# A row-sum kernel whose first row per partition becomes a block of its own: 128 contiguous rows, then blocks of 111 and 16 rows per partition

## The chip, the cores and the metric

The kernel runs on one core of a Trainium2 chip. The metric is device time in microseconds (us), the median of repeated runs. The profile comes from one further execution.

## The reference

```python
batch, seq, dim = 32, 512, 1024
x = np.random.randn(batch, seq, dim).astype(np.float32)

def reference(x):
    return np.sum(x, axis=-1).astype(np.float32)
```

There are 32 x 512 = 16384 rows of 1024 float32 numbers (4 KB a row, 67.1 MB in all), and the output is one float32 sum for each row.

## The kernel before

The 16384 rows are spread over 128 partitions, 128 rows to a partition, in two blocks. In the body block partition p holds the 112 consecutive rows from 112p on (`x_a`, `out_a`); in the end block it holds the 16 rows from 128 x 112 + 16p on (`x_z`, `out_z`). So two neighbouring partitions of the body lie 112 rows, 448 KB, apart in device memory, and two of the end block 64 KB.

The body is loaded in seven steps of 16 rows per partition (8.39 MB) into three buffers `xt0` to `xt2` in turn. Each step is two loads from SyncE's queue (SP), one for the even and one for the odd partitions, 64 partitions each, both counted on the semaphore of the buffer (`slots`). Step 0 is split once more: a small load of the first row of each partition (128 x 1024, semaphore `first`) goes ahead, and the two large loads bring the other 15 rows. The end block is loaded in pieces of 9, 4 and 2 rows (`CUTS`) into the next buffer, and its last row in two parts of 544 and 480 columns into `tail`. All 20 loads are issued by one loop (L138) in this order; from step 3 on SP waits until VectorE (DVE) has freed the buffer (`freed`, counted on `vec`). The first three loads (`EARLY = 3`) are moved by hand ahead of the barrier at the program's start.

VectorE waits for `first`, then for each step in turn, and reduces the 16 rows of a step with one instruction (L55) into `res_a`. Of step 6 it takes 9 rows, and ScalarE (ACT) takes the other 7, one instruction a row (L66). ScalarE then waits for all of these and issues the stores of `res_a` (L115) as three DMAs of 104, 12 and 12 partitions. Its part of the end block is behind these in its program: 5 of the 9 rows of piece 0, 2 of the 4 rows of piece 1, and 1 of the 2 rows of piece 2. VectorE takes the other rows; the last two rows are halved and added in pairs (L73), the very last one in its two parts. SP waits for ScalarE's and VectorE's counts (L139, L140), issues the store of `res_z` (L141), waits for `early_store`, clears the semaphores and waits for its store (L146).

```python
for i, k in ((0, 104), (104, 116), (116, P)):
    nc.scalar.dma_start(out=out_a[i:k], in_=res_a[i:k]).then_inc(sems["early_store"], 16)
```

Of the kernel before, what the change touches and what calls it, by code (L numbers as in the profile page):

```python
# [6 lines left out]
COPY = mybir.ActivationFunctionType.Copy  # L7
X = mybir.AxisListType.X

BODY = 112  # L10
G = 16
BUFS = 3
ACT_ROWS = 7
CUT = 544
# [4 lines left out]
def row_sums(nc, x: bass.AP, out: bass.AP):  # L19
    P = nc.NUM_PARTITIONS  # L20
    x_flat = x.flatten_outer_dims()
    R, D = x_flat.shape
    C = R // P
    assert R % P == 0 and C == BODY + G and BODY % G == 0
    out_flat = out.rearrange("a (b c) -> (a b c)", c=1)

    def block(r0, n):
        x_b = x_flat[r0 : r0 + P * n].rearrange("(p c) d -> p (c d)", p=P)
        out_b = out_flat[r0 : r0 + P * n].rearrange("(p c) -> p c", p=P)
        return x_b, out_b  # L30

    x_a, out_a = block(0, BODY)
    x_z, out_z = block(P * BODY, G)

    def sbuf(name, n):
        return nc.alloc_sbuf_tensor(name, [P, n], F32)

    xt = [sbuf(f"xt{i}", G * D) for i in range(BUFS)]
    tail = sbuf("tail", D + 16)
    pairs = [sbuf(f"pairs{i}", D // 2) for i in range(3)]  # L40
    res_a = sbuf("res_a", BODY)
    res_z = sbuf("res_z", G)

    names = [f"slot{i}" for i in range(BUFS)] + ["first", "piece0", "piece1", "piece2", "tail0"]
    names += ["tail1", "vec", "act", "early_store", "store"]
    sems = {n: nc.alloc_semaphore(n) for n in names}
    slots = [sems[f"slot{i}"] for i in range(BUFS)]
    vec, act = sems["vec"], sems["act"]
    numbers = [s.num for s in sems.values()]
    assert numbers == list(range(numbers[0], numbers[0] + len(numbers)))  # L50

    count = {"vec": 0, "act": 0}

    def rows_dve(t, j, n, res, c):
        nc.vector.tensor_reduce(  # L55
            out=res[:, c : c + n],
            in_=t[:, j * D : (j + n) * D].rearrange("p (j d) -> p j d", d=D),
            axis=X,
            op=ADD,
        ).then_inc(vec, 1)  # L60
        count["vec"] += 1

    def rows_act(t, j, n, res, c):
        for i in range(n):
            v = t[:, (j + i) * D : (j + i + 1) * D]
            nc.scalar.activation(  # L66
                out=v, in_=v, func=COPY, accum_out=res[:, c + i : c + i + 1]
            ).then_inc(act, 1)
            count["act"] += 1

    def pairs_dve(t, a, b, acc, pairs):
        h = (a + b) // 2
        nc.vector.tensor_tensor_reduce(  # L73
            out=pairs[:, 0 : h - a], in0=t[:, a:h], in1=t[:, h:b], scale=1.0, scalar=0.0,
            op0=ADD, op1=ADD, accum_out=acc,
        ).then_inc(vec, 1)
        count["vec"] += 1

    n_bufs = BODY // G


    freed = {}
    loads = []
    for b in range(n_bufs):
        c = b * G
        parts = [(q, 0, slots[b % BUFS]) for q in (slice(0, P, 2), slice(1, P, 2))]
        if b == 0:
            parts = [(slice(0, P), 0, sems["first"])] + [(q, 1, s) for q, i, s in parts]
        for q, i, s in parts:
            k = 1 if s is sems["first"] else G  # L90
            loads.append((b, xt[b % BUFS][q, i * D : k * D], x_a[q, (c + i) * D : (c + k) * D], s))
    last = xt[n_bufs % BUFS]
    for k, (i, j) in enumerate(zip(CUTS, CUTS[1:])):
        loads.append((n_bufs, last[:, i * D : j * D], x_z[:, i * D : j * D], sems[f"piece{k}"]))
    for k, (i, j, gap) in enumerate(((0, CUT, 0), (CUT, D, 16))):
        e = (G - 1) * D
        loads.append((0, tail[:, i + gap : j + gap], x_z[:, e + i : e + j], sems[f"tail{k}"]))


    nc.vector.memset(tail[:, CUT + 15 : CUT + 16], 0.0).then_inc(vec, 1)  # L100
    count["vec"] += 1
    nc.vector.wait_ge(sems["first"], 16)
    for b in range(n_bufs):
        a = ACT_ROWS if b == n_bufs - 1 else 0
        nc.vector.wait_ge(slots[b % BUFS], 32 * (b // BUFS + 1))
        rows_dve(xt[b % BUFS], 0, G - a, res_a, b * G)
        freed[b] = count["vec"]
        if a:
            nc.scalar.wait_ge(slots[b % BUFS], 32 * (b // BUFS + 1))
            rows_act(xt[b % BUFS], G - a, a, res_a, b * G + G - a)  # L110
    body_vec, body_act = count["vec"], count["act"]
    nc.scalar.wait_ge(vec, body_vec)
    nc.scalar.wait_ge(act, body_act)
    for i, k in ((0, 104), (104, 116), (116, P)):
        nc.scalar.dma_start(out=out_a[i:k], in_=res_a[i:k]).then_inc(sems["early_store"], 16)  # L115

    for k in range(2):
        i, j = CUTS[k], CUTS[k + 1]
        h = (j - i) // 2
        nc.vector.wait_ge(sems[f"piece{k}"], 16)  # L120
        rows_dve(last, i, h, res_z, i)
        nc.scalar.wait_ge(sems[f"piece{k}"], 16)
        rows_act(last, i + h, j - i - h, res_z, i + h)
    nc.scalar.wait_ge(sems["piece2"], 16)
    rows_act(last, 14, 1, res_z, 14)
    nc.vector.wait_ge(sems["piece2"], 16)
    pairs_dve(last, 13 * D, 14 * D, res_z[:, 13:14], pairs[2])
    nc.vector.wait_ge(sems["tail0"], 16)
    pairs_dve(tail, 0, CUT, tail[:, CUT + 14 : CUT + 15], pairs[0])
    nc.vector.wait_ge(sems["tail1"], 16)  # L130
    nc.vector.wait_ge(vec, count["vec"])  # L131
    pairs_dve(tail, CUT + 14, D + 16, res_z[:, 15:16], pairs[1])


    for b, dst, src, s in loads:
        if b >= BUFS:
            nc.sync.wait_ge(vec, freed[b - BUFS])
        nc.sync.dma_start(out=dst, in_=src).then_inc(s, 16)  # L138
    nc.sync.wait_ge(vec, count["vec"])  # L139
    nc.sync.wait_ge(act, count["act"])  # L140
    nc.sync.dma_start(out=out_z, in_=res_z[:, :]).then_inc(sems["store"], 16)  # L141


    nc.sync.wait_ge(sems["early_store"], 48)
    nc.sync.sem_clear(range(numbers[0], sems["store"].num))
    nc.sync.wait_ge(sems["store"], 16).then_inc(sems["store"], -16)  # L146


def kernel(tc: tile.TileContext, x: bass.AP, out: bass.AP):
    tc.close()  # L150
    tc.compile()  # L151
    nc = tc.nc
    row_sums(nc, x, out)

    sp = mybir.EngineType.SP
    fn = nc.m.functions[0]
    entry, body = None, None
    for blk in fn.blocks:  # L160
        ops = [i for i in blk.instructions if i.engine == sp]
        if entry is None:
            entry = blk
        elif any(i.opcode == "DMACopy" for i in ops):
            body = blk
            break
    code = list(body.instructions)
    loads = [i for i in code if i.engine == sp and i.opcode == "DMACopy"][:EARLY]
    for load in loads:
        assert not load.sync_info.on_wait  # L170
        code.remove(load)
    body.instructions = code
    code = list(entry.instructions)
    at = next(k for k, i in enumerate(code) if i.engine == sp and i.opcode == "Drain")
    code[at:at] = loads
    entry.instructions = code
# [29 lines left out]
```

## Time and profile before

| | |
|---|---|
| median of 3 runs | 160.85 us (160.85 to 160.98) |
| the profiled execution's own time | 160.87 us |
| its span in the profile | 159.5 us |
| DVE busy | 121.3 us (76%), 16 instructions |
| ACT busy | 17.1 us (11%), 31 instructions |
| DMA | 67.18 MB, mean 421 GB/s over the span |
| SP's queue (q1) | 2128 packets, 97.8% of 16 engines' span |
| ACT's queue (q10) | 165 packets, 0.1% |

The span runs from the first recorded instruction to the last one; the rest of the execution's time, 160.87 - 159.5 = 1.3 us, lies around it. A q1 packet is one partition's piece of a load (or of the last store), or the 4-byte write that counts the load as complete on one of the 16 DMA engines. "Idle before" an instruction tells how long its engine waited, and for what.

### The profile page before, as it was taken

Reading aid. Unit: us, or ns where it says so; the run is one execution under the profiler, and the core shown is the slowest. Engines: PE = TensorE matmul, PEld = TensorE weight load, DVE = VectorE, ACT = ScalarE, POOL = GpSimd, SP = SyncE. Lnnn points to the kernel's source line nnn. Section 1 sums busy time; section 2 is a strip of 40 time slices with the busy share of each in tenths; the row PEclk is TensorE's granted clock in tenths of the full one; section 3 lists DMA queues with packets and bytes.
Section 4 is the critical chain, followed back from the end, with each engine's and each line's share of the span. In section 5 each row is a group of like instructions: output and inputs, shape, how many; then the busy total and the mean of one; then the engine's idle time right before and its main releaser. Section 6 shows DMA issues by size and latency. Waiting matters only on the chain.

```text
span 159.5 us, 116 instructions
## 1 busy us (share of the span) xinstructions
DVE 121.3 (76%) x16; ACT 17.1 (11%) x31; POOL 0.2 (0%) x4
## 2 busy tenths in 40 slices
DVE  0000049998699968999599994999949999499785
ACT  2000000000000000000000000000000000394595
POOL 0000000000000000000000000000000000000000
DMA  9979996996996989979969969969969979799993
GB/s 378 493 308 431 493 509 279 526 509 279 526 493 296 526 378 411 526 329 460 526 296 493 526 279 509 526 263 526 509 279 526 460 329 526 305 434 444 395 411 131
DMA packets 2293, 67.18 MB, mean 421 GB/s; under 512 B 629, under 2 KB 757, under 8 KB 1013
## 3 DMA queue, kind: packets, MB, share of 16 engines
q1 hardware_dynamic: 2128, 67.12, 97.8%
q10 hardware_dynamic: 165, 0.06, 0.1%
HBM read 67.11 MB, written 0.07 MB: 421 GB/s over the span
## 4 chain that ended last, share of the span: by engine, by line
DMA 73%; DVE 23%; SPq 1%; issue 0%; DVEq 0%
DMA xt<-in_x_dram 73%; DVE res_a L55 22%; SPq L138 1%; DVE pairs L73 1%; DVEq L131 0%; DVE tail L73 0%; DVE res_z L73 0%
## 5 line engine op out<-in xcount | busy, mean ns | idle before, releaser
L55 DVE TENSOR_REDUCE res_a<-xt 128x16 f32<-128x16384 f32 (+1 forms) x7 | 113.1, 16153 | 31.7 <-DMA xt<-in_x_dram 31.7
L66 ACT ACTIVATE xt<-xt 128x1024 f32<-128x1024 f32 x15 | 15.6, 1041 | 137.7 <-DMA xt<-in_x_dram 137.7
L55 DVE TENSOR_REDUCE res_z<-xt 128x4 f32<-128x4096 f32 (+1 forms) x2 | 6.7, 3353 | 1.6 <-DMA xt<-in_x_dram 1.6
L66 ACT ACTIVATION_READ_ACCUMULATOR xt<-xt 128x1 f32 x15 | 2.8, 186 | 0.0
L100 DVE MEMSET tail<- 128x1 f32 x1 | 0.1, 59 | 3.0 <-PEq L151 3.0
L66 ACT ACT_TABLE_LOAD x1 | 1.3, 1283 | 2.9 <-PEq L151 2.9
L73 DVE CUSTOM_DVE_ANT_0 pairs<-tail 128x272 f32<-128x272 f32 (+1 forms) x2 | 0.8, 424 | 0.1
L73 DVE CUSTOM_DVE_ANT_0 pairs<-xt 128x512 f32<-128x512 f32 x1 | 0.7, 694 | 0.3 <-DMA xt<-in_x_dram 0.3
L73 DVE DVE_READ_ACCUMULATOR2_ANT res_z<- 128x1 f32 x2 | 0.2, 82 | 0.0
L190 POOL MEMSET const-bfloat16-1.0<- 128x1 bf16 x1 | 0.1, 101 | 0.0
L190 POOL MEMSET const-uint8-127<- 128x1 uint8 x1 | 0.1, 101 | 0.0
L190 POOL MEMSET const-float32-0.0<- 128x1 f32 x1 | 0.1, 98 | 0.2 <-issue 0.2
L190 POOL MEMSET const-float32-1.0<- 128x1 f32 x1 | 0.1, 98 | 0.0
L73 DVE DVE_READ_ACCUMULATOR2_ANT tail<- 128x1 f32 x1 | 0.1, 82 | 0.0
## 6 DMA issues: line engine op xcount, KB each, us to landing
xt<-in_x_dram SPq DMA_DIRECT2D x2, 3840.0 KB, 16.6
xt<-in_x_dram SPq DMA_DIRECT2D x1, 4608.0 KB, 32.4
xt<-in_x_dram SPq DMA_DIRECT2D x1, 2048.0 KB, 36.9
xt<-in_x_dram SPq DMA_DIRECT2D x1, 1024.0 KB, 39.0
xt<-in_x_dram SPq DMA_DIRECT2D x1, 512.0 KB, 3.8
tail<-in_x_dram SPq DMA_DIRECT2D x1, 272.0 KB, 39.1
tail<-in_x_dram SPq DMA_DIRECT2D x1, 240.0 KB, 39.2
xt<-in_x_dram SPq DMA_DIRECT2D x12, 39.0
```

The costliest lines, as they stand in the source:

```text
L55: nc.vector.tensor_reduce(out=res[:, c : c + n], in_=t[:, j * D : (j + n) * D].rearrange("p (j d) -> p j d", d=D), axis=X, op=ADD,).then_i ...
L66: nc.scalar.activation(out=v, in_=v, func=COPY, accum_out=res[:, c + i : c + i + 1]).then_inc(act, 1)
L73: nc.vector.tensor_tensor_reduce(out=pairs[:, 0 : h - a], in0=t[:, a:h], in1=t[:, h:b], scale=1.0, scalar=0.0, op0=ADD, op1=ADD, accum_out ...
L100: nc.vector.memset(tail[:, CUT + 15 : CUT + 16], 0.0).then_inc(vec, 1)
L138: nc.sync.dma_start(out=dst, in_=src).then_inc(s, 16)
L190: nc = _bacc.Bacc("TRN2", target_bir_lowering=False, num_devices=1)
```

## The change

The first row of each partition is taken out of the body. A new block, `x_h` and `out_h`, holds rows 0 to 127 of the whole input, one to a partition, so that its load reads 512 KB that lie in one piece. The body starts at row 128 with 111 rows per partition (steps of 15, 16, 16, 16, 16, 16, 16 rows); the end block stays where it was. VectorE reduces the new block with an instruction of its own into `res_h`, and step 0 then has 15 rows instead of 16. ScalarE issues a fourth store, `res_h` to `out_h` (128 partitions, 4 bytes each), behind the three of `res_a`, and `early_store` is waited for at 64 instead of 48. The neighbouring partitions of the body lie 444 KB apart instead of 448 KB. Number, order and sizes of the 20 loads stay the same.

```diff
-BODY = 112
+BODY = (15, 16, 16, 16, 16, 16, 16)
+HEAD = 1
+END = 16
...
-    x_a, out_a = block(0, BODY)
-    x_z, out_z = block(P * BODY, G)
+    x_h, out_h = block(0, HEAD)
+    x_a, out_a = block(P * HEAD, N)
+    x_z, out_z = block(P * (HEAD + N), END)
...
-        c = b * G
+        c = starts[b]
         parts = [(q, 0, slots[b % BUFS]) for q in (slice(0, P, 2), slice(1, P, 2))]
-        if b == 0:
-            parts = [(slice(0, P), 0, sems["first"])] + [(q, 1, s) for q, i, s in parts]
+        m = HEAD if b == 0 else 0
+        if m:
+            loads.append((b, xt[b][:, 0 : m * D], x_h, sems["first"]))
         for q, i, s in parts:
-            k = 1 if s is sems["first"] else G
-            loads.append((b, xt[b % BUFS][q, i * D : k * D], x_a[q, (c + i) * D : (c + k) * D], s))
+            k = BODY[b]
+            loads.append((b, xt[b % BUFS][q, m * D : (m + k) * D], x_a[q, c * D : (c + k) * D], s))
...
     nc.vector.wait_ge(sems["first"], 16)
+    rows_dve(xt[0], 0, HEAD, res_h, 0)
     for b in range(n_bufs):
         a = ACT_ROWS if b == n_bufs - 1 else 0
         nc.vector.wait_ge(slots[b % BUFS], 32 * (b // BUFS + 1))
-        rows_dve(xt[b % BUFS], 0, G - a, res_a, b * G)
+        rows_dve(xt[b % BUFS], 0 if b else HEAD, BODY[b] - a, res_a, starts[b])
...
     for i, k in ((0, 104), (104, 116), (116, P)):
         nc.scalar.dma_start(out=out_a[i:k], in_=res_a[i:k]).then_inc(sems["early_store"], 16)
+
+    nc.scalar.dma_start(out=out_h, in_=res_h[:, :]).then_inc(sems["early_store"], 16)
...
-    nc.sync.wait_ge(sems["early_store"], 48)
+    nc.sync.wait_ge(sems["early_store"], 64)
```

## The prediction

> **What bounds the kernel now.** I read the page's queues and chain first, then the timeline of the end, then the start in windows of 0.25 us, and last the packet records behind these views. Queue and chain:
>
> ```profile
> q1 hardware_dynamic: 2128, 67.12, 97.8%
> q10 hardware_dynamic: 165, 0.06, 0.1%
> DMA xt<-in_x_dram 73%; DVE res_a L55 22%; SPq L138 1%; DVE pairs L73 1%; DVEq L131 0%; DVE tail L73 0%; DVE res_z L73 0%
> ```
>
> SP's load queue keeps all 16 DMA engines at work for 97.8% of the span. The chain also names the VectorE reductions (L55), but that is only because a freed buffer releases an issue. The next lines show that these releases cost nothing:
>
> ```profile
> 41.25 17.22 DVE L55 TENSOR_REDUCE res_a<-xt 128x16 f32<-128x16384 f32 x1 [2.06 <-DMA xt<-in_x_dram]
> 60.60 17.22 DVE L55 TENSOR_REDUCE res_a<-xt 128x16 f32<-128x16384 f32 x1 [2.13 <-DMA xt<-in_x_dram]
> ...
> 149.22 1.06 ACT L66 ACTIVATE xt<-xt 128x1024 f32<-128x1024 f32 x1 [3.83 <-DMA xt<-in_x_dram]
> ...
> 157.46 0.18 ACT L66 ACTIVATION_READ_ACCUMULATOR xt<-xt 128x1 f32 x1
> 157.63 0.41 DVE L73 CUSTOM_DVE_ANT_0 pairs<-tail 128x241 f32<-128x241 f32 x1
> 157.97 0.08 DVE L73 DVE_READ_ACCUMULATOR2_ANT res_z<- 128x1 f32 x1
> 158.08 0.35 SPq L141 DMA_DIRECT2D out_dram<-res_z  x1
> ```
>
> VectorE waits 2.1 us for every step: 8.39 MB each 19.35 us, 433 GB/s. In the packet records a 65,536-byte packet takes 2.418 us at the median (27.1 GB/s an engine, 433.6 GB/s for 16), a 61,440-byte one 2.267, and packets follow one another without gaps from about 3 us to 157.08. So the end is fixed by when the slowest engine gets into its stride, plus the bytes, plus whatever else it carries. Behind that comes a tail: the last load lands 39.2 us after its issue at 118.35, at 157.55; VectorE's last pair of rows starts at 157.63 and ends at 158.05; SP's store follows at 158.08. ScalarE ends at 157.64, so it has 0.4 us to spare.
>
> The start is the only stretch where the engines are not in stride:
>
> ```profile
> 0.75:1.00 0.25, 0.00 (x0) 0.00 (x0) 0.00 (x0) 1.00 0.00 0
> 1.00:1.25 0.25, 0.00 (x0) 0.00 (x0) 0.00 (x0) 1.00 1.62 164
> 1.25:1.50 0.25, 0.00 (x0) 0.00 (x0) 0.00 (x0) 1.00 0.53 82
> 1.50:1.75 0.25, 0.00 (x0) 0.00 (x0) 0.00 (x0) 1.00 0.26 98
> 1.75:2.00 0.25, 0.00 (x0) 0.00 (x0) 0.00 (x0) 1.00 0.80 246
> 2.00:2.25 0.25, 0.00 (x0) 0.00 (x0) 0.00 (x0) 1.00 1.06 393
> 2.25:2.50 0.25, 0.00 (x0) 0.00 (x0) 0.00 (x0) 1.00 1.03 426
> ```
>
> The last column is GB/s, counted by packets in the stretch where they start. From 1.0 to 2.0 us it is 82 to 246 instead of over 400. This is the 128-packet first load. Its records: 4096 bytes take 159 ns at the median, but 218 ns in the mean and up to 994 ns; the slow ones are each engine's first packets, which start between 1.02 and 1.43 us. The excess is 8 x (218.3 - 159) ns = 0.47 us per engine in the mean. The 16 completions of this load spread from 2.63 to 3.40 us; the latest engine stalled twice (842 and 591 ns) and ends last at 157.08 too.
>
> **The change part by part.**
>
> **The contiguous first load.** It is still 128 packets of 4096 bytes, 8 to an engine, and SP issues it in the same place, so issue (0.38 us) and bytes stay. What moves is the addresses: engines read 32 KB apart within 512 KB, instead of one row every 448 KB. An engine ends 157.08 - 3.40 = 153.68 us after its first completion if it carries no store. An engine that carries stores takes 8.84 - 8.65 = 0.19 us longer from piece 0's completions to the last load's (147.91 to 156.75 against 148.43 to 157.08). 104 rows lie on 13 engines and 12 on 12 (128 rows + 37 completions = the 165 packets of q10), so three engines have none.
> Without stalls a first completion comes at 1.02 + 8 x 0.159 = 2.29 us for the first engine and 1.43 + 1.27 = 2.70 for the last. If all the stall stays, it comes at 3.40 as now. Does the stall come from scattered addresses, or from a cold start that any first packet meets? For addresses: the latest engine's very first packet (at 1.015, 156 ns) was quick, and its second and third, 448 KB on each, were not. Against: at 136.8 us the end block's untouched memory is entered, and the first 36,864-byte packets keep to 1.364 to 1.372 us; there, though, work was queued ahead. I take half of the mean stall as staying: 2.70 + 0.24 = 2.94 for the latest engine.
>
> [...]
>
> **The fourth store, on the DMA engines.** 128 packets of 4 bytes and 16 completions, 9 per engine. The nearest rows are the 4-byte completions, 9 ns, and the 64-byte packets of the `res_z` store, 8 to 11 ns: 9 x 9 = 0.08 us per engine. Below zero is excluded, since the packets stand between loads on busy engines. The upper end is the 448-byte packets' 25 ns: 0.23 us. I take 0.08, the row nearest in size. Rows of `res_a` become 444 instead of 448 bytes, for which I add nothing up to 10 x 25 ns = 0.25 us should a packet double. The queue alternates with SP's: the present stores run from 151.2 to 155.76, and the new packets then fit between the 16 packets of the two tail loads (88 and 79 ns), so they are done by about 156.7. SP looks at `early_store` only at 158.48, so that wait is covered by some 1.5 us.
>
> [...]
>
> **The fourth store, on ScalarE.** The three issues take 1.38 us from 147.79 and already hold ScalarE until 149.22, though piece 0 was there for VectorE at 148.92. From there ScalarE goes without a pause to 157.64, so the new issue delays everything queued behind it: 8 rows, and SP's L140 that waits for them. Nearest rows: 0.31, 0.38 and 0.62 us for the three, 0.35 for the 128-partition store of `res_z`. I take 0.38 + 0.03 between issues = 0.41; ends 0.34 and 0.65. ScalarE then ends at 158.05 (157.98 to 158.29) against VectorE's 158.05: nothing to +0.25 us, and nothing taken, because the cover of 0.40 us is just used up. A gain at the start moves both ends alike.
>
> **VectorE.** One more reduction of one row at about 4 us, 1.1 to 1.2 us by 9.75 us for 9 rows and 2.29 for 2. It lies inside the 18.96 us that VectorE waits for step 0. Step 0's reduction becomes 17.22 - 1.08 = 16.14 us. SP's issue of step 3, at 39.22, comes some 1.1 us earlier; nobody waits, since the engines reach step 3 only at 59.4, when step 2's completions come. Nothing.
>
> **The body at 444 KB pitch.** Packet counts and sizes are equal. Rows now start on multiples of 4 KB instead of 64 KB; so do the 61,440-byte packets and the pieces now, and they run at 27 GB/s. Nothing; no gain either, since no packet has a gap to give up. The price if wrong is the slower rival.
>
> Sum: latest store engine 2.94 + 0.19 + 0.08 + 153.68 = 156.89 against 157.08, -0.19 us; the tail follows. 160.87 - 0.19 = 160.68 for the profiled execution, 160.66 by the median, which is 0.02 lower; I say 160.65.
>
> **Rivals.**
> *The stall moves or stays.* The stretches after the contiguous load are new memory for step 0's 60 KB rows, and the stall could fall there, or it was a cold start. For it: ten or more of the 16 first packets were slow, whatever their address. Then only the store's 0.08 us is left, at most 0.25 with ScalarE last: 160.95.
> *All of the stall goes.* 2.70 + 0.19 + 0.08 + 153.68 = 156.65, -0.43 us: 160.4.
> *Slower: the rows that no longer start on 64 KB.* Place: the 56 body packets of each engine behind the first load. Single 65,536-byte packets reach 2.462 us, 44 ns over the median. At 10 ns each it costs 0.56 us: 161.4. It outweighs the forecast gain from 3.4 ns a packet, and is slower by over 0.2% from about 9. Against it: the 4 KB-aligned packets of today show nothing.
>
> **How the numbers follow.** A measurement of this kernel tells about 0.2%, 0.32 us, from no change: below 160.53, above 161.17. Forecast 0.45 (160.45 to 160.85, of which 0.11 under 160.53); all goes 0.22; stays or moves 0.18 (0.03 over 161.17); slower 0.15 (0.14 over). Faster 0.33, within 0.50, slower 0.17. The range 160.3 to 161.2 leaves out most of the slower case and the edge of the second rival.
>
> **What would show it.** Right: the first load's completions before 3.0 us, step 0's reduction starting about 0.2 to 0.5 us earlier than 21.98 and every later one by as much, q10 at 309 packets, ScalarE's first end-block row at about 149.6 less that shift, and VectorE and ScalarE ending within 0.2 us of each other. Wrong: 60 KB packets over 2.3 us (the stall moved), 64 KB packets over 2.43 us and steps further apart than 19.35 us (the pitch), or a ScalarE that ends after VectorE by 0.2 us or more.

## The result, and the profile after

The changed kernel takes 166.85 us (median of 6 runs, 166.0 to 167.48) where the kernel before takes 160.88 (160.85 to 161.03): slower, ratio 1.0367 with a 95% interval of 1.035 to 1.0383. The forecast was 160.65 with a range of 160.3 to 161.2.

The profiled execution took 167.48 us, its span is 166.1. The page's queues and chain of the changed kernel:

```profile
q1 hardware_dynamic: 2128, 67.12, 94.2%
q10 hardware_dynamic: 309, 0.06, 0.2%
DMA xt<-in_x_dram 48%; DMA tail<-in_x_dram 27%; DVE res_a L60 21%; SPq L148 1%; DVE pairs L78 1%; DVEq L141 0%; DVE tail L78 0%; DVE res_z L78 0%
```

Bytes and q1 packets are the same, but SP's queue fills 94.2% of the span instead of 97.8%, and the chain now ends in a wait for the `tail` loads, which before had no share of it. The timeline shows two losses. The first is at the start (lines of VectorE; L60 is the reduction that was L55; the line with L55 is the kernel before's step 0, whose next two lines stand in the prediction):

```profile
21.98 17.22 DVE L55 TENSOR_REDUCE res_a<-xt 128x16 f32<-128x16384 f32 x1 [18.96 <-DMA xt<-in_x_dram]
...
3.44 1.22 DVE L60 TENSOR_REDUCE res_h<-xt 128x1 f32<-128x1024 f32 x1 [0.41 <-DMA xt<-in_x_dram]
23.20 16.15 DVE L60 TENSOR_REDUCE res_a<-xt 128x15 f32<-128x15360 f32 x1 [18.54 <-DMA xt<-in_x_dram]
42.55 17.22 DVE L60 TENSOR_REDUCE res_a<-xt 128x16 f32<-128x16384 f32 x1 [3.20 <-DMA xt<-in_x_dram]
61.90 17.22 DVE L60 TENSOR_REDUCE res_a<-xt 128x16 f32<-128x16384 f32 x1 [2.13 <-DMA xt<-in_x_dram]
```

Step 1 starts at 42.55 instead of 41.25, 1.3 us late, step 2 at 61.90 instead of 60.60, and so on: the steps keep their 19.35 us. So this loss arises in step 0 and is carried to the end. The second loss is at the end (again the line of the kernel before first, L73, which is now L78):

```profile
157.04 0.44 DVE L73 CUSTOM_DVE_ANT_0 pairs<-tail 128x272 f32<-128x272 f32 x1
...
155.15 2.29 DVE L60 TENSOR_REDUCE res_z<-xt 128x2 f32<-128x2048 f32 x1 [0.48 <-DMA xt<-in_x_dram]
158.69 0.69 DVE L78 CUSTOM_DVE_ANT_0 pairs<-xt 128x512 f32<-128x512 f32 x1 [1.25 <-DMA xt<-in_x_dram]
159.30 0.08 DVE L78 DVE_READ_ACCUMULATOR2_ANT res_z<- 128x1 f32 x1
163.64 0.44 DVE L78 CUSTOM_DVE_ANT_0 pairs<-tail 128x272 f32<-128x272 f32 x1 [4.26 <-DMA tail<-in_x_dram]
164.24 0.41 DVE L78 CUSTOM_DVE_ANT_0 pairs<-tail 128x241 f32<-128x241 f32 x1 [0.15 <-DVE tail L78]
164.69 0.35 SPq L151 DMA_DIRECT2D out_dram<-res_z  x1
```

Piece 1 is still 1.33 us late (155.15 against 153.82), piece 2 2.27 (158.69 against 156.42), and the first part of the last row 6.60 (163.64 against 157.04). VectorE waits 4.26 us for it. In these windows of the changed kernel (stretch, its length, busy time of DVE, ACT and POOL, clock, DMA share, GB/s) the DMA engines have nothing left to move meanwhile:

```profile
159.00:160.00 1.00, 0.39 (x2) 0.83 (x2) 0.00 (x0) 1.00 0.03 10
160.00:161.00 1.00, 0.00 (x0) 0.00 (x0) 0.00 (x0) 1.00 0.00 0
161.00:162.00 1.00, 0.00 (x0) 0.00 (x0) 0.00 (x0) 1.00 0.00 0
162.00:163.00 1.00, 0.00 (x0) 0.00 (x0) 0.00 (x0) 1.00 0.00 0
```

The data has been moved, but it has not been reported: a load has landed when the semaphore that it is counted on has the completions of all 16 DMA engines. In the packet records the last completion of the first tail load starts at 158.77 and takes 9 ns; its count is full at 163.62. For the second one the records reach 159.38, with one completion that took 3821 ns instead of 9, and its count is full at 163.98. Before, the second count was full at 157.52, 0.44 us after its last packet. The counts of the fourth store itself come in until 163.80. The issues of the changed kernel, with us to landing, show it on the page, first before, then after:

```profile
tail<-in_x_dram SPq DMA_DIRECT2D x1, 272.0 KB, 39.1
tail<-in_x_dram SPq DMA_DIRECT2D x1, 240.0 KB, 39.2
...
tail<-in_x_dram SPq DMA_DIRECT2D x1, 272.0 KB, 44.4
tail<-in_x_dram SPq DMA_DIRECT2D x1, 240.0 KB, 44.3
```

### The profile page after: what moved, and what is told of

Read it like the earlier page. It is cut to its first block, busy times and chain, and to the rows that moved or that the text cites. A ratio compares the mean times of both kernels' runs of the same rounds, so it can differ in the third digit from the quotient of the medians.

```text
span 166.1 us, 117 instructions
## 1 busy us (share of the span) xinstructions
DVE 121.6 (73%) x17; ACT 17.2 (10%) x31; POOL 0.2 (0%) x4
## 3 DMA queue, kind: packets, MB, share of 16 engines
q1 hardware_dynamic: 2128, 67.12, 94.2%
## 4 chain that ended last, share of the span: by engine, by line
DMA 75%; DVE 21%; SPq 1%; issue 0%; DVEq 0%
DMA xt<-in_x_dram 48%; DMA tail<-in_x_dram 27%; DVE res_a L60 21%; SPq L148 1%; DVE pairs L78 1%; DVEq L141 0%; DVE tail L78 0%; DVE res_z L78 0%
## 5 line engine op out<-in xcount | busy, mean ns | idle before, releaser
L60 DVE TENSOR_REDUCE res_a<-xt 128x16 f32<-128x16384 f32 (+2 forms) x7 | 112.0, 16001 | 32.4 <-DMA xt<-in_x_dram 32.4
L60 DVE TENSOR_REDUCE res_z<-xt 128x4 f32<-128x4096 f32 (+1 forms) x2 | 6.7, 3353 | 1.7 <-DMA xt<-in_x_dram 1.7
L78 DVE CUSTOM_DVE_ANT_0 pairs<-tail 128x272 f32<-128x272 f32 (+1 forms) x2 | 0.9, 427 | 4.4 <-DMA tail<-in_x_dram 4.3
L78 DVE CUSTOM_DVE_ANT_0 pairs<-xt 128x512 f32<-128x512 f32 x1 | 0.7, 693 | 1.2 <-DMA xt<-in_x_dram 1.2
L60 DVE TENSOR_REDUCE res_h<-xt 128x1 f32<-128x1024 f32 x1 | 1.2, 1220 | 0.4 <-DMA xt<-in_x_dram 0.4
L78 DVE DVE_READ_ACCUMULATOR2_ANT res_z<- 128x1 f32 x2 | 0.2, 82 | 0.0
L78 DVE DVE_READ_ACCUMULATOR2_ANT tail<- 128x1 f32 x1 | 0.1, 83 | 0.0
```

The costliest lines, as they stand in the source:

```text
L60: nc.vector.tensor_reduce(out=res[:, c : c + n], in_=t[:, j * D : (j + n) * D].rearrange("p (j d) -> p j d", d=D), axis=X, op=ADD,).then_i ...
L78: nc.vector.tensor_tensor_reduce(out=pairs[:, 0 : h - a], in0=t[:, a:h], in1=t[:, h:b], scale=1.0, scalar=0.0, op0=ADD, op1=ADD, accum_out ...
```

## The experiments

They ran in five sets, each beside runs of the kernel before: 161.69, 161.39, 161.50, 161.70 and 161.88 us there. The kernel before was less even in these sets than in its first runs (160.59 to 163.59), and that spread is itself part of the start's story below; so each number is compared within its set. Packets and lines of a version are those of one profiled execution; where its own time lies far from the median, it is given.

Theory STORE: the fourth store delays the completions of the tail. Rival LATE ENGINE: the engines that are late from the start explain all.

**no_h_store**: no fourth store.

```diff
-    nc.scalar.dma_start(out=out_h, in_=res_h[:, :]).then_inc(sems["early_store"], 16)
```

> The changed kernel without its fourth store (rows 0 to 127 of the output stay unwritten). Theory STORE: the 128 writes of 4 bytes into one 512-byte stretch of device memory are slow to finish, and the completions of the tail loads wait behind them on the same DMA engines; without them the tail lands 0.5 us after its last packet, and only the late start is left (step 6 lands 1.3 us later than before): 162.2 us. Rival LATE ENGINE: two engines that stalled at the start are late by up to 1.4 us and carry the whole loss to the end; the time stays at 166 to 167 us.

Measured: 162.05 us against 161.69, ratio 1.002 (0.9992 to 1.0048). The end of its profile, VectorE's lines and then the tail's landings:

```profile
158.10 0.43 DVE L78 CUSTOM_DVE_ANT_0 pairs<-tail 128x272 f32<-128x272 f32 x1
158.70 0.41 DVE L78 CUSTOM_DVE_ANT_0 pairs<-tail 128x241 f32<-128x241 f32 x1
```

```profile
tail<-in_x_dram SPq DMA_DIRECT2D x1, 272.0 KB, 39.2
tail<-in_x_dram SPq DMA_DIRECT2D x1, 240.0 KB, 39.3
```

No wait for the tail is left, and the landings are those of before. LATE ENGINE falls: most of the loss is the store's. What is left over the kernel before, 0.36 us, is not clear of the noise in this run.

**after_again**: the changed kernel unaltered, as a yardstick in set 2.

> The changed kernel unaltered, beside the others of this set. It is the yardstick for the stores: by theory STORE, 4 to 5 us over its version without the fourth store (162.05 where the kernel before was 161.69), so 3% over the kernel before; the tail loads' last completions land 4 us or more after their last packet.

Measured: 166.7 us against 161.39, ratio 1.0314 (1.024 to 1.0388). Over its set's kernel before that is 5.3 us; the version without the store is 0.36 over its own. So the store costs about 4.95 us, a difference between two sets. The tail's last count comes 3.3 us after its last packet in this profile, less than the 4 us expected.

**column_store**: the kernel before, with 128 x 4 bytes that go 448 bytes apart.

```diff
-    ...dma_start(out=out_a[i:k], in_=res_a[i:k])
+    ...dma_start(out=out_a[i:k, 1:], in_=res_a[i:k, 1:])
+    nc.scalar.dma_start(out=out_a[:, 0:1], in_=res_a[:, 0:1], ...).then_inc(sems["early_store"], 16)
```

> The kernel before, with a fourth store of 128 x 4 bytes in the same place, but the 4 bytes of each partition go 448 bytes apart (column 0 of the body's sums; the three stores write columns 1 to 111). If each 4-byte write to device memory is slow by itself, the tail's completions land some 4 us late and the time is about 165 us. If it is the 128 writes into one 512-byte stretch that are slow, the tail lands as before and the time is 160.9 to 161.2 us.

Measured: 161.25 us against 161.69, ratio 0.9992 (0.9958 to 1.0026). Same number of packets, same size, same queue and place: no cost that these runs tell from nothing, and the tail's last count comes 0.33 us after its last packet. A write of 4 bytes is not slow by itself.

**h_store_64**: the changed kernel, 4-byte writes 64 bytes apart.

```diff
-    for i, k in ((0, 104), (104, 116), (116, P)):
+    for i, k in ((0, 104),):
...
-    nc.scalar.dma_start(out=out_h, in_=res_h[:, :])
+    d = out_flat[11680 : 11680 + 16 * P].rearrange("(p c) -> p c", p=P)[:, 0:1]
+    nc.scalar.dma_start(out=d, in_=res_h[:, :], ...)
```

> The changed kernel with the 128 writes of 4 bytes 64 bytes apart instead of 4 (into output rows that are left free by leaving out the two stores of 12 partitions; rows 0 to 127 stay unwritten). If the cost is that many writes fall on the same 64 bytes, the tail lands 0.5 us after its last packet and the time is 162 to 162.5 us, that of no fourth store. If it is that they fall close together in device memory at all, or on a few neighbouring stretches, 164 to 167 us.

Measured: 163.09 us (161.51 to 163.49) against 161.39, ratio 1.0074 (1.0021 to 1.0126). The time is above the first band, but not by the store. The tail of its profile:

```profile
tail<-in_x_dram SPq DMA_DIRECT2D x1, 272.0 KB, 39.2
tail<-in_x_dram SPq DMA_DIRECT2D x1, 240.0 KB, 39.3
```

The second part's count was full 0.4 us after its last packet. What is left is the start: step 0 was complete at 23.92 us (21.52 before). So the cost needs writes that lie closer together than 64 bytes.

**h_store_16**: only 16 of the 128 writes, all in one 64-byte line.

```diff
-    nc.scalar.dma_start(out=out_h, in_=res_h[:, :])
+    nc.scalar.dma_start(out=out_h[0:16], in_=res_h[0:16, :])
```

> The changed kernel whose fourth store writes only 16 partitions (16 writes of 4 bytes, all into one 64-byte line; rows 16 to 127 stay unwritten). If every write to a shared line waits for the one before it, the cost goes with the number of writes on a line: one line's 16 writes take as long as each of the eight lines' 16 would by itself, so 4 us and 166 us if lines are worked on side by side, but an eighth, about 0.5 us and 162 to 164 us, if all 128 go through one place in turn.

Measured: 161.92 us against 161.50, ratio 1.0039 (0.9998 to 1.008); last count 0.27 us after its last packet. One 64-byte line's 16 writes leave nothing to see, so it is not that each of the eight lines takes the 4 us by itself, side by side. But here each DMA engine has one write (the queue has 32 packets more than the three stores' 165, 16 of them completions), where it has eight in the changed kernel; whether the cost goes with the writes of an engine or with those of all engines is the question of early_8x16.

**early_h_store**: the store right after the new block's reduction, at about 5 us.

```diff
     rows_dve(xt[0], 0, HEAD, res_h, 0)
+    nc.scalar.wait_ge(vec, count["vec"])
+    nc.scalar.dma_start(out=out_h, in_=res_h[:, :]).then_inc(sems["early_store"], 16)
...
-    nc.scalar.dma_start(out=out_h, in_=res_h[:, :]).then_inc(sems["early_store"], 16)
```

> The changed kernel with the fourth store issued by ScalarE at the start, as soon as VectorE has reduced the new block (about 5 us), instead of behind the three stores of the body. STORE, if the writes only hurt when a completion that matters stands behind them: they pass between 2.3 us load packets, one at a time per engine, nothing waits for step 0 before 23 us, and the time is that without the store, 162.2 us. STORE, if slow writes hold the engines themselves: part of the 4.3 us comes back at the start, 163 to 166 us. LATE ENGINE: 166 to 167 us.

Measured: 165.3 us against 161.69, ratio 1.0207 (1.017 to 1.0245). The tail lands in time now, but VectorE's first steps do not:

```profile
26.56 16.15 DVE L60 TENSOR_REDUCE res_a<-xt 128x15 f32<-128x15360 f32 x1 [22.14 <-DMA xt<-in_x_dram]
45.74 17.22 DVE L60 TENSOR_REDUCE res_a<-xt 128x16 f32<-128x16384 f32 x1 [3.02 <-DMA xt<-in_x_dram]
```

Step 0 is taken up at 26.56 us instead of 23.20. In the packet records, 65,536-byte load packets take up to 3.48 us instead of 2.42 between 23 and 27 us, where the last of the small writes stand. The writes do not only delay completions, they hold the engines.

**early_8x16**: the same, in eight DMAs of 16 partitions, so that an engine's eight writes go to eight different lines.

```diff
-    nc.scalar.dma_start(out=out_h, in_=res_h[:, :]).then_inc(sems["early_store"], 16)
+    for i in range(0, P, 16):
+        nc.scalar.dma_start(out=out_h[i : i + 16], in_=res_h[i : i + 16, :]).then_inc(sems["early_store"], 16)
```

> The version with the fourth store issued at the start (165.3 us, step 1's packets up to 3.48 us), that store cut into eight DMAs of 16 partitions: the same 128 writes of 4 bytes into the same 512 bytes, but each engine's eight writes now go to eight different 64-byte lines. Theory PER ENGINE (an engine's write to a line waits for its own last write to that line): no cost left, 161.7 to 162.7 us, 65,536-byte packets under 2.6 us. Theory ONE PLACE (all writes into the stretch are taken one after the other): about as before, 164.5 to 166 us.

Measured: 166.14 us against 161.70, ratio 1.028 (1.0227 to 1.0332). VectorE's first two steps, in the profile of an execution of 167.82 us:

```profile
26.74 16.15 DVE L60 TENSOR_REDUCE res_a<-xt 128x15 f32<-128x15360 f32 x1 [22.20 <-DMA xt<-in_x_dram]
48.03 17.22 DVE L60 TENSOR_REDUCE res_a<-xt 128x16 f32<-128x16384 f32 x1 [5.14 <-DMA xt<-in_x_dram]
```

PER ENGINE, which expected no cost, falls: not less than in one DMA, and packets of up to 3.7 us. Of the two, ONE PLACE is left. It is not shown cleanly: the eight DMAs also bring 128 completions instead of 16, one behind each write, and what these add was not run by itself.

**transposed_store**: the complete change, with VectorE turning the 128 sums into four rows of 32.

```diff
-    res_h = sbuf("res_h", HEAD)
+    res_h = sbuf("res_h", 32)
+    res_t = sbuf("res_t", 32)
...
+    nc.vector.transpose(out=res_t[:, :], in_=res_h[:, :]).then_inc(vec, 1)
...
-    nc.scalar.dma_start(out=out_h, in_=res_h[:, :])
+    nc.scalar.dma_start(out=out_flat[0:P].rearrange("(a c) -> a c", a=4), in_=res_t[0:P:32, :])
```

> The changed kernel, complete, with the new block's sums transposed in blocks of 32 x 32 by VectorE, so that the fourth store is four packets of 128 bytes instead of 128 of 4. By both theories of the store its cost goes: the tail lands 0.5 us after its last packet, 161.7 to 162.7 us. What is left over the kernel before, 0.3 to 1 us, is the start.

Measured: 163.49 us (161.63 to 163.62, four runs) against 161.70, ratio 1.0104 (1.0037 to 1.017). The tail lands 0.4 us after its last packet, as expected; the time is above the band, because step 0 was complete only at 23.96 us. With its store mended, the change still loses at the start (three of the four runs are at 163.49 to 163.62, one is at 161.63).

The start. Theory TOUCH: the first access to memory stalls, and the scattered first load meets it with small packets. Rival PITCH: the 444 KB.

**contig_first**: the kernel before, only the source of the first load contiguous.

```diff
+            src = x_a[q, (c + i) * D : (c + k) * D]
+            if s is sems["first"]:
+                src = block(0, 1)[0]
...
```

> The kernel before, with only the source of the small first load changed: it reads rows 0 to 127 of the input in one stretch (so the first sum of each partition is of a wrong row); body, pitch of 448 KB and stores as before. Theory TOUCH: the scattered first load meets the untouched memory of all partitions with small packets, and without it the 61,440-byte packets of step 0 stall instead: some of them take over 2.7 us, step 6 lands about 1 us later, 161.5 to 162.3 us. Rival PITCH (the 444 KB pitch stalls step 0): packets of step 0 stay at 2.27 us, and the time is 160.4 to 160.9 us.

Measured: 162.43 us against 161.69, ratio 1.0049 (1.0012 to 1.0086). In its profile, of an execution of 163.52 us, packets of step 0 reach 3.95 us, with a mean of 2.390 instead of 2.267, and step 0 is taken up late:

```profile
24.55 17.22 DVE L55 TENSOR_REDUCE res_a<-xt 128x16 f32<-128x16384 f32 x1 [21.52 <-DMA xt<-in_x_dram]
43.83 17.22 DVE L55 TENSOR_REDUCE res_a<-xt 128x16 f32<-128x16384 f32 x1 [2.06 <-DMA xt<-in_x_dram]
```

**pitch_444**: the kernel before with the body at 444 KB and the scattered first load.

```diff
+            r = P + c + i
+            src = x_flat[r : r + P * 111].rearrange("(p c) d -> p (c d)", p=P)
+            src = src[q, 0 : (k - i) * D]
...
```

> The kernel before, with the body's partitions 444 KB apart and starting at row 128, and the scattered first load kept (rows overlap by one between partitions, so bytes and packets are as before and the body's sums are of other rows). Theory TOUCH: no effect, the ratio to the kernel before is 1.000 within 0.004. Rival PITCH: step 0's packets stall as in the changed kernel, ratio 1.004 to 1.008; or, if the pitch hurts every step, steps over 19.35 us apart and a ratio over 1.01.

Measured: 161.76 us against 161.39, ratio 1.0016 (0.9972 to 1.006). Step 0's packets have a mean of 2.270 us, in the profile of an execution of 160.64 us. PITCH has no support, and contig_first shows a loss at the old pitch; but the interval reaches 1.006, so a small share of the pitch is not ruled out.

**no_first**: no small first load.

```diff
-EARLY = 3
+EARLY = 2
...
-        if b == 0:
-            parts = [(slice(0, P), 0, sems["first"])] + [(q, 1, s) for q, i, s in parts]
...
-    nc.vector.wait_ge(sems["first"], 16)
```

> The kernel before without the small first load: step 0 is loaded as 16 whole rows per partition. TOUCH: the first accesses now stall packets of 65,536 bytes; step 0's packets reach 3 us and more, and the time is 0.5 to 1.3 us over the kernel before. Rival: the first load is of no use, and its own slow packets go with it: 0.2 to 0.5 us under the kernel before.

Measured: 161.28 us (161.2 to 161.46) against 161.39, ratio 1.0 (0.9973 to 1.0028). Each engine's first packet takes 2.45 to 3.25 us instead of 2.42, but then all are in stride: the second ones start from 4.26 us on and take 2.43 to 2.44. The stall of TOUCH is there, its price is not, and the time is remarkably even.

**touch_then_contig**: the version without the fourth store, and ahead of all loads 64 bytes from each partition's body rows.

```diff
+            loads.append((b, xt[b][:, D : D + 16], x_a[:, 0:16], sems["first"]))
             loads.append((b, xt[b][:, 0 : m * D], x_h, sems["first"]))
...
```

> The changed kernel without its fourth store, with one more load ahead of all others: the first 64 bytes of each partition's body rows (128 packets at 444 KB), which step 0 then leaves out. Theory TOUCH (what stalls is the first access to a stretch of memory, and it is cheap if small packets meet it all over first): step 0's packets stay near 2.27 us, step 0 is in by 21.3 to 22.0 us where the versions with the contiguous load alone took 22.4 to 24.1, and the time is 160.8 to 161.7 us. Rival COLD START (the contiguous load itself, or what follows any first load, stalls): step 0 in at 22.4 to 24 us, 162 us or more.

Measured: 162.17 us against 161.50, ratio 1.0028 (0.9993 to 1.0063). The 128 small packets are recorded with 8 to 11 ns each and all are through by 1.37 us; step 0 then still has packets of up to 3.36 us and is complete at 22.67. TOUCH falls in the form tested: that each partition's rows have been met at their first 64 bytes does not keep step 0 from stalling.

**touch_16 and touch_128**: the kernel before with 16 or 128 columns in the first load.

```diff
-            loads.append((b, xt[b % BUFS][q, i * D : k * D], x_a[q, (c + i) * D : (c + k) * D], s))
+            e = 16 if s is sems["first"] else G * D
+            loads.append((b, xt[b % BUFS][q, i * 16 : e], x_a[q, c * D + i * 16 : c * D + e], s))
```

> The kernel before with the small first load cut from 1024 to 16 columns (64 bytes from each partition's first row; step 0's loads bring the rest). TOUCH: the same stretches are met by shorter packets, whose stalls can overlap; step 0 in by 21.0 to 21.5 us (before 21.52), time 0 to 0.6 us under the kernel before. Rival: the 4 KB of the first load are needed as cover while the next packets' accesses run ahead; step 0's packets stall as without a first load, step 0 in at about 21.75, time as before or up to 0.5 us over.

> The kernel before with the small first load cut from 1024 to 128 columns (512 bytes from each partition's first row). Between the other two: TOUCH gives 0 to 0.6 us under the kernel before, with step 0 in by 21.0 to 21.5 us; the rival gives up to 0.4 us over.

Measured: 161.75 us (161.66 to 161.94), ratio 1.0028 (1.0007 to 1.005), and 161.66 us, ratio 1.0017 (0.9983 to 1.005). Behind the short first loads, most engines' first large packet takes about 3 us, as without a first load; step 0 is complete at 22.24 and 22.22 us, later than any of the times expected.

**scatter_far**: the first load reads row 56 of each partition.

```diff
+            r = 56 if s is sems["first"] else c + i
```

> The kernel before with the small first load reading row 56 of each partition's 112 instead of row 0: 448 KB apart as before, but 224 KB away from what step 0 reads next (the first sum of each partition is of a wrong row). Theory NEIGHBOUR (the first load prepares the ground for step 0's rows because it lies beside them): step 0's packets stall as behind the contiguous load, mean 2.31 us or more, step 0 in at 22.4 to 24 us, ratio 1.003 to 1.009. Theory SCATTER (only that the 128 rows lie apart matters): mean under 2.31 us, step 0 in at 21.3 to 22.2 us, ratio 1.000 within 0.003.

Measured: 161.81 us against 161.70, ratio 1.0004 (0.9969 to 1.0038), mean of step 0's packets 2.296 us; complete at 22.28, between the two bands. With one profile and a value between the bands, SCATTER is only favoured; NEIGHBOUR has no support from the time.

**first_2rows**, and **first_2rows_again**: the kernel before with two rows per partition in the first load.

```diff
-            parts = [(slice(0, P), 0, sems["first"])] + [(q, 1, s) for q, i, s in parts]
+            parts = [(slice(0, P), 0, sems["first"])] + [(q, 2, s) for q, i, s in parts]
...
-            k = 1 if s is sems["first"] else G
+            k = 2 if s is sems["first"] else G
```

> The kernel before with two rows of each partition in the small first load (packets of 8192 bytes) and 14 in step 0's two loads. If the stall of the first reads is met in the first load and is then over, step 0's packets run at 27.1 GB/s in every run; the slow ones among the runs of the kernel before (over 162 us) go, and the median is 0.2 to 0.6 us lower, 160.7 to 161.1. Rival: the stall has nothing to do with the first load's length, and median and spread stay.

> The kernel before with two rows of each partition in the small first load, once more in five rounds: 160.97 in ten runs where the kernel before had 161.70. If the gain is real, the median is again 0.3 to 0.8 us under the kernel before of the same set, with a spread under 1 us, and the interval of the ratio stays under 1.

Measured: 160.97 us against 161.70, ratio 0.9966 (0.9939 to 0.9994), and 160.85 (160.65 to 161.26) against 161.88, ratio 0.9933 (0.991 to 0.9956). This version beats both kernels, by being even: the kernel before ran from 160.83 to 163.59 in that set. Against the 160.88 of the kernel before's even first runs it is no gain.

**contig_2rows**: the same with a contiguous source of 1 MB.

```diff
+            if s is sems["first"]:
+                src = block(0, 2)[0]
```

> The kernel before with a first load of two rows per partition whose source is one stretch of 1 MB (rows 0 to 255, so the first two sums of each partition are of wrong rows), and 14 rows per partition in step 0's loads. Theory LENGTH (the start is slow for some 3 to 4 us, whatever is read): the longer load covers it, step 0's packets of 57,344 bytes run at 2.116 us as behind the scattered two rows, 160.7 to 161.2 us. Theory ADDRESSES (only scattered addresses take the stall upon themselves): step 0's packets stall again, up to 3 us, 162 us or more.

Measured: 160.96 us (160.86 to 161.12) against 161.88, ratio 0.9947 (0.9926 to 0.9967). Packets of the first load reach 1.23 us instead of the usual 0.31, those of step 0 run at 2.117 in the mean and never over 2.131. VectorE's first steps, in contig_2rows:

```profile
21.86 17.22 DVE L55 TENSOR_REDUCE res_a<-xt 128x16 f32<-128x16384 f32 x1 [18.85 <-DMA xt<-in_x_dram]
41.17 17.22 DVE L55 TENSOR_REDUCE res_a<-xt 128x16 f32<-128x16384 f32 x1 [2.09 <-DMA xt<-in_x_dram]
```

ADDRESSES falls: a contiguous first load of two rows, which lasts until 4.06 to 4.51 us, leaves step 0 as undisturbed as a scattered one. LENGTH forecast this, but its reason, a start that is slow for 3 to 4 us whatever is read, does not fit contig_first: there packets that start between 4 and 6 us still take up to 3.95 us, while in no_first those from 4.26 us on are in stride.

The profiles side by side bear out the rest. With one scattered row, step 0's last completion starts at 21.28 to 22.28 us (before, pitch_444, column_store, scatter_far); with one contiguous row, at 21.94 to 24.11 (after, after_again, no_h_store, h_store_64, h_store_16, transposed_store, contig_first). The start is uneven in both, and more so with the contiguous row.

## Why the prediction was wrong

**Fourth store, on the DMA engines: the step that failed.** The prediction priced it by its packets, 9 x 9 ns = 0.08 us, at most 0.23, and put it beside the tail loads. The packets did take 9 ns each. But the price was not in them: it was in when the writes end, and the working took the record of a packet for the end of its write. They cost about 4.95 us (after_again and no_h_store). "The row nearest in size" was the wrong nearness: a completion does not go to the output, a 64-byte packet of `res_z` has 64 bytes of it to itself, and the 128 new writes share 512. Durations could give no upper bound; that needed landings of such a store, and the trace of before has none. What makes writes so close together slow was not shown; h_store_64, h_store_16 and early_8x16 only say that they must be closer than 64 bytes, that 16 in one line show nothing, and that spreading an engine's eight over the lines did not help.

The Trainium skill (page "DMA: Bandwidth & Descriptors", section "Queues, rings and completion order") says that a completion is a strongly ordered write, which lands only after every earlier write of that engine, across its queues. This trace agrees: a completion recorded at 158.77 us was counted only at 163.62, behind another queue's writes. With this rule weighed, the placing of the store among the last loads was the risk to look at. The same page ("Specifications") puts 512 bytes as the least size for full rate, with read-modify-write below; here 4-byte writes 448 bytes apart and packets of 128 bytes cost nothing, so size alone does not decide.

**First load.** The prediction let half of the mean stall stay and the rest go, a gain of 0.19 us. For the first load itself that was close: its last completion starts at 3.02 us (2.80 to 3.31 in the other profiles with one contiguous row), against 2.94 forecast and 3.40 before. What failed is the next term, that an engine ends 153.68 us after its first completion: step 0's packets stalled instead. The case "the stall moves or stays", with 0.18 of the chances, was the nearest. The prediction named its sign: 60 KB packets over 2.3 us. They reach 3.31 in the changed kernel, and two of the 16 engines finish the even half of step 0 at 13.19 and 13.76 us where the last one did so at 12.46 before. But that case priced no extra delay, and the loss is 1.3 us in the profile, 0.74 by contig_first's medians, 0.36 by no_h_store's. Of the two reasons given for it, new memory found no support in touch_then_contig; a cold start fits no_first's first packets, but not alone the later ones of contig_first. That the engines read 32 KB apart was a guess, since no run shows which rows an engine takes; no term of the sum rests on it. And the slow packets before were not only first ones that start by 1.43 us: four more, of 262 to 591 ns, start between 1.80 and 2.03.

**ScalarE.** The issue was priced at 0.38 us and took 0.37 in the changed kernel:

```profile
150.50 0.37 ACTq L125 DMA_DIRECT2D out_dram<-res_h  x1
150.91 1.06 ACT L71 ACTIVATE xt<-xt 128x1024 f32<-128x1024 f32 x1 [4.23 <-DMA xt<-in_x_dram]
```

It cost nothing: VectorE's wait for the tail hides it. **VectorE** was right: 1.22 us for the new row, 16.15 for step 0, both covered. **The pitch** was right in the forecast (nothing that pitch_444 tells from noise) and has no support as the slower rival: the kernel did get slower, but the steps kept their 19.35 us. **The wait for `early_store`** was to be covered by 1.5 us; the store's counts came in at 163.80, where its packets were to be done by about 156.7, and only because all else was late too did SP, at 165.09, find them there.

Open: why one contiguous row leaves the engines so uneven. That it is over too early (first completions from 2.33 to 2.80 us in contig_first, 2.63 to 3.40 before) fits contig_2rows, but not touch_16 and touch_128, whose first loads are over by 1.5 us and which lose less (ratios 1.0028 and 1.0017 against 1.0049, step 0 complete at 22.2 us against 24.11). Also open is where between 512 bytes and 8 KB for 128 writes the store's cost ends, and the change with two rows in its head and a transposed store was not tried.

## What to carry to other kernels

Price a store by when its writes are counted as landed, and ask whose completions stand behind it on the same DMA engines; sums that lie one to a partition are better transposed into a few packets before they are stored. In a kernel bound by its loads, look at how evenly the 16 engines get into stride: a first load of two rows per partition, in packets of 8 KB until about 4 us, was worth 0.3 to 0.7% here beside the kernel before of the same set, scattered or contiguous. And where a change adds a small thing beside a moved big one, run each alone: here the small one cost most.

## What the runs showed of the hardware

128 writes of 4 bytes into 512 bytes took from about 154.1 us (the first 4-byte packets of ScalarE's queue) to 163.8 (their last counts) in the changed kernel, an estimate of at most (163.8 - 154.1) / 128 = 76 ns each if they go one after another, though each packet is recorded with 9 ns; meanwhile completions of other loads were held back by up to 4.9 us. 128 such writes 64 or 448 bytes apart held nothing back (h_store_64, column_store).

The first large packets that the engines read were slow (up to 3.25 us instead of 2.42 in no_first, up to 1.23 instead of 0.31 in contig_2rows), while 128 packets of 64 bytes were recorded with 8 to 11 ns each, all within 0.4 us (touch_then_contig).
